# A down projection of seven products in place of eight, with sums of its weights made by accumulating DMAs

## The chip, the cores and the metric

The kernel runs on one core of one Trainium2 chip. The metric is the device time of one launch in microseconds (us), the median of several executions.

## What is computed

One step of a hybrid streaming encoder layer on 640 tokens (512 of a new stream, 8 streams of 16), all in float32, with a model width of 2048:

```python
proj = x @ w_in + b_in                            # 2048 -> 6144: conv and HGRN2 groups
mixed = concat(conv_mixer(proj), hgrn2_mixer(proj)) @ w_out
h = layer_norm(ALPHA * x + mixed)
ffn = (silu(h @ w_gate) * (h @ w_up)) @ w_down    # 2048 -> 5632 -> 2048
y = layer_norm(ALPHA * h + ffn)
```

The conv mixer is a causal convolution of 31 taps over 1024 channels with a carried history; the HGRN2 mixer a gated recurrence of 8 heads with a carried state.

## The kernel before

Channels lie on the partitions and tokens on the free dimension, in two halves of 320 (`TH`). A float32 product is made of three float32r matmuls (`mac`, lines 222 to 227): weights and operand are each split into a high and a low part (`part`, lines 156 and 157: ACT casts the high part, DVE subtracts to get the low one), and high x high, high x low and low x high are added up in PSUM.

Weights come through one feed. `take` gives the next piece of up to 512 columns as four tiles of 128 x 128 and prepares those behind it; `feed_weights` loads up to 1024 columns at a time (`raw`, three buffers, line 206) on SP's queue. The order of TensorE, DVE and ACT is the order of the program text; the orders of POOL and SP are set by a scheduler. After a group of matmuls, `tick` runs steps of side work (mixers, norms).

The stages, one after another on TensorE:

- Input projection, with the mixers as side work. `MIXERS` sets the order: c0 c1 h0 c2 h1 c3 c4 h2 c5 h3 and so on, c for a conv tile and h for a head. For each conv tile POOL clears the head of `u` (line 318), loads the history into a `tmp` buffer (line 320), copies it into `us` (line 321), and later stores the new history (lines 335 to 338). DVE then runs the taps over `u` and `us` (lines 360 and 362). For each head POOL loads the state (line 449), spreads the streams' queries into `qm` (line 542) and stores the new states (lines 563 and 578). The four `tmp` buffers go round among histories, gates, squares (line 580) and normed outputs (line 591).
- Output projection, residual, first norm.
- SwiGLU: the gate and up products in Winograd's form of Strassen's algorithm, seven products of a quarter of the size in place of eight (`quad`); sums of their weights are made on DVE (line 879). Results go to DRAM as `act_d`.
- Down projection, 5632 to 2048, in the plain form: 44 hidden tiles in six chunks (`CHUNKS`). For the first four chunks (`down`), a weight tile serves both halves of the tokens; the last two (`down_half`) go through all 16 output tiles for the first half of the tokens and then again for the second, so their weights are loaded and split twice. The operands of a chunk are loaded from `act_d` on POOL's queue (line 951) and split during the chunk before (`stage`). Sums over the chunks are added to the residual `res`, reloaded from `h_d`, on DVE (lines 1027, 1029, 1052, 1071).
- Second norm (`pivot`, `norm2`), that of the first half under the products of the second.

A semaphore named DMASW0 to DMASW7 belongs to each DMA of POOL's queue in turn, so an issue there waits until the DMA eight before it is done.

Of the kernel before, what the change touches and what calls it, by code (L numbers as in the profile page):

```python
# [10 lines left out]
F32 = mybir.dt.float32  # L11
# [60 lines left out]
def kernel(ctx, tc, xT, cacheT, s_in, w_in, w_out, w_last, w_gate, w_up, w_down,  # L72
# [53 lines left out]
    # Side work (the mixers, the norms) runs after each group of matmuls: a step of each lane, and as many  # L126
    # steps of the fillers as fit in the time (us of VectorE; each step yields what it takes).
# [26 lines left out]
    def part(src, hi, lo, lows=None):  # L154
        """src as hi + lo. lows: takes what VectorE has to do, for later."""
# [8 lines left out]
    # The feed holds, in the order of their use, functions that give up to 512 columns of weights.  # L164
# [7 lines left out]
    def take(ahead=None):  # L172
        """The next weights as (hi, lo) of P columns each; the ones after them are prepared ahead."""
# [22 lines left out]
    def feed_weights(*srcs, offset=2500):  # L196
        """Each up to 1024 columns of weights in all; an item of the feed for each 512."""
        raws = []

        def raw():  # L200
            if not raws:
                with tc.high_priority(offset=offset):
                    t = wp.tile([P, 1024], F32, tag="raw", name="raw")
                    j = 0
                    for src in srcs:
                        nc.sync.dma_start(t[:, j:j + src.shape[-1]], src)
                        j += src.shape[-1]
# [3 lines left out]
        total = sum(src.shape[-1] for src in srcs)  # L211
# [4 lines left out]
    def split(kt, half, src, lows=None):  # L216
        hi = xp.tile([P, TH], F32R, tag=f"xh{kt}_{half}", name="xh")
        lo = xp.tile([P, TH], F32R, tag=f"xl{kt}_{half}", name="xl")
        part(src, hi, lo, lows)
        return hi, lo  # L220
# [30 lines left out]
    def first_pair(outs):  # L251
        """The first two output tiles together, in the order in which x arrives."""
# [49 lines left out]

    mixed = {}
# [72 lines left out]
    def mean_of(t, out, n):  # L376
        """Sum over the partitions / D of the n columns of t, in all partitions."""
# [176 lines left out]
        # states  # L554
# [12 lines left out]
        # outputs, tokens on the partitions  # L567
# [30 lines left out]
    def stream_blocks(t):  # L598
        """The block of LB columns of each stream, out of its own P columns."""
# [212 lines left out]
    # weights^T = [[a11, a12], [a21, a22]] (output tiles x channels), h = [[b11, b12], [b21, b22]]  # L812
# [24 lines left out]
    # What follows the products, a little after each of the next ones: (us of VectorE, function).  # L837
# [15 lines left out]
    def early(store):  # L853
        """The two products that need the first half of the tokens alone."""
# [58 lines left out]
    def quad(stored, c11, c12, c21, c22, upper, lower):  # L913
        """upper, lower: what follows when c11 and c12, when c21 and c22 are there."""
# [22 lines left out]
        for s in range(2):  # L937
            for i in sum(groups, ()):
                product(bank[i], operand[i], s)
                if s == 1:  # L940
                    later.extend(sums.get(i, []))
        later.append((0.7, lower))

    act_d = [dp.tile([P, NTOK], F32, name=f"act_d{ft}") for ft in range(FT)]
# [9 lines left out]
    def split_act(c, i, t):  # L954
        return [split(2 * i + h, c % 2, half(t, h)) for h in range(2)]

    def feed_down(c, n):
        feed_weights(w_down[n, :, P * CHUNKS[c][0]:P * sum(CHUNKS[c])])

    def swiglu(j):  # L960
# [12 lines left out]
        def store(e):  # L973
            vec.tensor_tensor(g[e], g[e], v[e], op=ALU.mult)
            pool.dma_start(act_d[2 * j + e], g[e])

        quad(stored[1], half(v[0], 0), half(v[0], 1), half(v[1], 0), half(v[1], 1),
             lambda: store(0), lambda: store(1))

    acts = []  # L980
    early_d = []
    for wq, stored in products:
        feed_quad(wq, stored)
    for c in range(NCHUNK - 2):
        for n in range(KD):
            feed_down(c, n)
    for h in range(2):
        for c in LAST:
            for n in range(KD):
                feed_down(c, n)  # L990
# [6 lines left out]
    for j in range(QUADS):  # L997
        swiglu(j)

# [1 line left out]
    def down_macs(c, n, outs, halves, between=None):  # L1001
        i = 0
# [244 lines left out]
```

## Time and profile before

| | |
|---|---|
| median of 3 runs | 2798.1 us (2797.22 to 2800.35) |
| profiled execution, span | 2797.9 us |
| TensorE, instructions | 18888 matmuls, each with its weight load |
| DMA, HBM read and written | 302.53 MB and 37.28 MB |
| weights on SP's queue (q1) | 276.42 MB, 31.5% of 16 engines' span |
| POOL's queue (q0) | 63.44 MB, 7.0% |
| loads of w_down | 112 of 512 KB, 16 of 256 KB |

The trace gives for an instruction its start, length, line, output and inputs, and in brackets the idle time of its engine before it with what ended it. PE is TensorE, PEld its weight loads, DVE VectorE, ACT ScalarE, POOL GpSimd, SP SyncE. The profiled execution's own time is not given apart from its span; the runs beside it lie within 2.5 us of that.

### The profile page before, as it was taken

To read this page: it belongs to the slowest core of one execution; us is meant where nothing else is said; L and a number is where in the kernel's file an instruction comes from. 1 tells how busy PE (TensorE), PEld (TensorE's weight loads), DVE (VectorE), ACT (ScalarE), POOL (GpSimd) and SP (SyncE) were. 2 spreads that over 40 slices of the span, in tenths; PEclk is the share of its full clock that TensorE was granted. 3 is DMA by queue.
4 is the path that set the end of the run, shared out by engine and by line. 5 is a ranking of instruction groups with operands and counts; after the bars stand their busy time and mean duration, and the time that the engine had idled before them with its cause. 6 is when DMAs were issued, how large, how long until landed. Compare 5 with 4: busy or idle time off the path is not lost.

```text
span 2797.9 us, 47299 instructions
## 1 busy us (share of the span) xinstructions
PE 2758.8 (99%) x18888; PEld 2740.3 (98%) x18888; DVE 1928.7 (69%) x3461; ACT 1005.1 (36%) x1706; POOL 155.3 (6%) x270
## 2 busy tenths in 40 slices
PE   8999999999999999999999999999999999999996
PEld 8999999999999999999999999999999999999996
DVE  7866876875665667788888777777776423335686
ACT  3222122222543466643333333343334212213444
POOL 1001000000000000100000000000001000000001
PEclk9999999999999999999999999999999999999998
DMA  5222222222225556754454323333336423334463
GB/s 187 65 79 90 64 87 79 82 77 70 74 88 170 173 165 205 259 169 156 158 158 156 107 89 105 102 95 104 99 104 230 135 74 111 97 91 128 140 180 103
DMA packets 104094, 342.89 MB, mean 123 GB/s; under 512 B 12992, under 2 KB 17600, under 8 KB 103872
## 3 DMA queue, kind: packets, MB, share of 16 engines
q1 hardware_dynamic: 87296, 276.42, 31.5%
q0 software_dynamic: 16576, 63.44, 7.0%
q8 instruction: 148, 2.42, 0.4%
q14 instruction: 74, 0.61, 0.1%
HBM read 302.53 MB, written 37.28 MB: 121 GB/s over the span
## 4 chain that ended last, share of the span: by engine, by line
PE 97%; DVE 1%; ACT 1%; DMA 0%; issue 0%; SPq 0%; ACTq 0%; DVEq 0%
PE psg L224 21%; PE psg L227 21%; PE psg L225 21%; PE psd L224 10%; PE psd L227 10%; PE psd L225 10%; PE psh L525 2%; PE psh L565 0%; PE psh L441 0%; PE psh L574 0%; PE psd L1151 0%; PE psh L570 0%; PE psh L504 0%; PE psh L498 0%; PE psh L557 0%; DVE res L1112 0%
## 5 line engine op out<-in xcount | busy, mean ns | idle before, releaser
L224 PE MATMUL psg<-xh,hi 128*128 128x320 f32 x3404 | 1050.1, 313 | 1.2 <-ACT xh L156 1.2
L225 PE MATMUL psg<-xl,hi 128*128 128x320 f32 x3404 | 1037.3, 309 | 1.2 <-DVE xl L157 1.2
L227 PE MATMUL psg<-xh,lo 128*128 128x320 f32 x3404 | 895.3, 310 | 2.9 <-DVE lo L157 2.8
L156 ACT CAST hi<-raw 128x512 fp32r<-128x512 f32 (+1 forms) x824 | 507.2, 619 | 1039.8 <-PE psg L225 715.9
L157 DVE TENSOR_TENSOR lo<-raw,hi 128x512 fp32r<-128x512 f32 (+1 forms) x824 | 560.3, 688 | 293.7 <-ACT hi L156 292.5
L224 PEld LDWEIGHTS psg<-xh,hi 128*128 128x128 f32 x3404 | 640.3, 188 | 4.2 <-issue 1.7
L225 PEld LDWEIGHTS psg<-xl,hi 128*128 128x128 f32 x3404 | 640.2, 188 | 3.9 <-issue 1.7
L227 PEld LDWEIGHTS psg<-xh,lo 128*128 128x128 f32 x3404 | 599.3, 188 | 5.3 <-DVE lo L157 5.2
L225 PE MATMUL psd<-xl,hi 128*128 128x320 f32 x1424 | 436.5, 309 | 0.0
L224 PE MATMUL psd<-xh,hi 128*128 128x320 f32 x1424 | 436.4, 309 | 0.0
L227 PE MATMUL psd<-xh,lo 128*128 128x320 f32 x1424 | 403.6, 309 | 0.0
L156 ACT CAST hi<-S 128x512 fp32r<-128x512 f32 x352 | 218.0, 619 | 356.5 <-PE psd L225 164.3
L157 DVE TENSOR_TENSOR lo<-S,hi 128x512 fp32r<-128x512 f32 x352 | 243.0, 690 | 116.5 <-ACT hi L156 109.7
L224 PEld LDWEIGHTS psd<-xh,hi 128*128 128x128 f32 x1424 | 267.3, 188 | 0.0
L225 PEld LDWEIGHTS psd<-xl,hi 128*128 128x128 f32 x1424 | 267.2, 188 | 0.0
L227 PEld LDWEIGHTS psd<-xh,lo 128*128 128x128 f32 x1424 | 258.1, 188 | 0.0
L224 PE MATMUL psg<-t,hi 128*128 128x320 f32 x624 | 192.8, 309 | 0.0
L225 PE MATMUL psg<-t,hi 128*128 128x320 f32 x624 | 192.8, 309 | 0.0
L227 PE MATMUL psg<-t,lo 128*128 128x320 f32 x624 | 192.8, 309 | 0.0
L362 DVE SCALAR_TENSOR_TENSOR mx<-u,par,mx 128x512 f32<-128x512 f32 x240 | 180.7, 753 | 0.0
L879 DVE TENSOR_TENSOR S<-raw 128x512 f32<-128x512 f32 x176 | 120.7, 686 | 24.8 <-DMA raw<-w_up 14.3
L224 PE MATMUL psd<-t,hi 128*128 128x320 f32 x432 | 133.5, 309 | 0.0
(228 smaller groups left out, 2707.6 us busy)
## 6 DMA issues: line engine op xcount, KB each, us to landing
raw<-w_down SPq DMA_DIRECT2D x112, 512.0 KB, 3.7
raw<-w_in SPq DMA_DIRECT2D x92, 512.0 KB, 3.8
raw<-w_gate SPq DMA_DIRECT2D x88, 512.0 KB, 3.5
raw<-w_up SPq DMA_DIRECT2D x88, 512.0 KB, 3.6
raw<-w_out SPq DMA_DIRECT2D x60, 512.0 KB, 3.9
act_d<-gu POOLq DMA_DIRECT2D x44, 320.0 KB, 2.5
act<-act_d POOLq DMA_DIRECT2D x42, 320.0 KB, 3.8
raw<-w_gate SPq DMA_DIRECT2D x40, 256.0 KB, 3.3
```

Source lines behind the costliest of these rows:

```text
L156: act.copy(hi, src)
L157: low = lambda: vec.tensor_tensor(lo, src, hi.bitcast(F32), op=ALU.subtract)
L224: pe.matmul(ps, w[0], xh, start=start, stop=False)
L225: pe.matmul(ps, w[0], xl, start=False, stop=False)
L227: pe.matmul(ps, w[1], xh, start=False, stop=stop)
L362: vec.scalar_tensor_tensor(y, x, col(w0 + j), y, op0=ALU.mult, op1=ALU.add)
L525: pe.matmul(ps[:, P // 2 * c:P // 2 * (c + 1)], blk(k, c), upper(q, c, m), start=True, stop=True)
L879: vec.tensor_tensor(t, x, y, op=op)
```

## The change

The down projection takes the seven-product form too: `w_down` is seen as pairs of output tiles (p, 0 to 7) by two halves of the hidden tiles (22 each), the activations as two halves of the hidden tiles by two halves of the tokens. The seven products run one after another (`DOWN`), each over all eight p: 22 weight tiles of 128 x 128 for each p, on one half of the tokens' width (320 columns), three matmuls each. Weights of products 1, 2 and 4 are quarters of `w_down`; those of 5, 7, 6 and 3 are sums of two, two, three and four quarters. The operands of a product are loaded from `act_d` (one to three pieces for each two tiles), subtracted on DVE, split, and put where operands of the product before are no longer needed (`prepare`, a filler). Each result is added to one or more quarters of `res` (`done1` and so on).

The sums of weights lie in DRAM (`s_d`). They are made by DMAs on POOL's queue, from DRAM to DRAM: a copy of one term, and then an accumulating DMA that adds another. There are 32 of each, and each is of 128 x 2816 float32. `tick` issues one at every second call, from the first tile of the input projection on.

```diff
-CHUNKS = [(0, 4), (4, 8), (12, 8), (20, 8), (28, 8), (36, 8)]
-NCHUNK = len(CHUNKS)
-LAST = (NCHUNK - 2, NCHUNK - 1)
...
+PAIRS_OUT = KD // 2
+DOWN = (1, 2, 6, 7, 4, 5, 3)
...
         while fillers and credit[0] > 0:
-            credit[0] -= fill()
+            cost = fill()
+            if cost is None:
+                break
+            credit[0] -= cost
+        ticks[0] += 1
+        if ticks[0] % 2:
+            next(summing, None)
+    ticks = [0]
...
+    HALF = QUADS * P
+    s_d = {i: [dp.tile([P, HALF], F32, name=f"s{i}_{p}") for p in range(PAIRS_OUT)] for i in (5, 7, 6, 3)}
+    def quarter_of(p, r, c):
+        return w_down[2 * p + r, :, HALF * c:HALF * (c + 1)]
+    def sum_weights(out, src, accumulate):
+        if accumulate:
+            pool.dma_start(out, src, accum_op=ALU.add, max_dma_last_dim=2 * HALF)
+        else:
+            pool.dma_start(out, src)
+    def weight_sums():
+        for terms in (lambda p: [(5, quarter_of(p, 1, 0), quarter_of(p, 1, 1)),
+                                 (7, quarter_of(p, 0, 0), quarter_of(p, 1, 0))],
+                      lambda p: [(6, s_d[5][p], quarter_of(p, 0, 0))],
+                      lambda p: [(3, s_d[6][p], quarter_of(p, 0, 1))]):
+            for n in range(2):
+                for p in range(PAIRS_OUT):
+                    for i, *two in terms(p):
+                        sum_weights(s_d[i][p], two[n], n == 1)
+                        yield
+    summing = weight_sums()
...
-    def raw_act(c, i):
-        if c == 0 and i < 2:
-            t = gp.tile([P, NTOK], F32, tag="pre", name="pre", bufs=2)
-        else:
-            t = sp.tile([P, NTOK], F32, tag=f"a{i}", name="act", bufs=1)
-        pool.dma_start(t, act_d[CHUNKS[c][0] + i])
-        return t
...
-    def feed_down(c, n):
-        feed_weights(w_down[n, :, P * CHUNKS[c][0]:P * sum(CHUNKS[c])])
+    act_d = [dp.tile([P, 2, NTOK], F32, name=f"act_d{j}") for j in range(QUADS)]
+    t2_d = [dp.tile([P, 2, TH], F32, name=f"t2_d{jj}") for jj in range(QUADS // 2)]
 
     def swiglu(j):
         stored = early_d[2 * j:2 * j + 2] if 2 * j < EARLY else [None, None]
...
+    ops = {i: [] for i in DOWN}
+    progress = [-1, 0, 0]
...
+    def loads(i, jj):
+        parts = {1: ("11",), 2: ("21",), 6: ("22", "12", "11"), 7: ("22", "12"), 4: ("t2", "21"),
+                 5: ("12", "11"), 3: ("22",)}[i]
+        out = []
+        for n, name in enumerate(parts):
+            if n == 0:
+                t = gp.tile([P, 2, TH], F32, tag="pre", name="pre", bufs=2)
+            elif n == 1:
+                t = sp.tile([P, 2, TH], F32, tag="xr", name="pre2")
+            else:
+                t = pair_tmp()
+            if name == "t2":
+                pool.dma_start(t, t2_d[jj])
+            else:
+                pool.dma_start(t, half3(act_d[jj + QUADS // 2 * (int(name[0]) - 1)], int(name[1]) - 1))
+            out.append(t)
+        return out
...
+    def prepare(i):
+        nth = DOWN.index(i)
+        got = deque([loads(i, 0)])
+        yield None
+        for jj in range(QUADS // 2):
+            if jj + 1 < QUADS // 2:
+                got.append(loads(i, jj + 1))
+            t, *others = got.popleft()
+            if i == 6:
+                b12, b11_ = others
+                vec.tensor_tensor(b12, b12, b11_, op=ALU.subtract)
+                yield 0.85
+            for o in others[:1]:
+                vec.tensor_tensor(t, t, o, op=ALU.subtract)
+                yield 0.85
+            if i == 6:
+                pool.dma_start(t2_d[jj], t)
+            while nth and (progress[0] < nth - 1 or jj > 8 and progress[0] == nth - 1 and
+                           (progress[1] < PAIRS_OUT - 1 or progress[2] < 2)):
+                yield None
+            hi, lo = space(), space()
+            act.copy(hi, t)
+            yield None
+            vec.tensor_tensor(lo, t, hi.bitcast(F32), op=ALU.subtract)
+            ops[i].extend((hi[:, e], lo[:, e]) for e in range(2))
+            yield 0.85
...
+    def down_weights(i, p, j, n):
+        w = {1: lambda: quarter_of(p, 0, 0), 2: lambda: quarter_of(p, 0, 1), 4: lambda: quarter_of(p, 1, 1)}
+        return (w[i]() if i in w else s_d[i][p])[:, P * j:P * (j + n)]
+    def runs(i):
+        if i == DOWN[0]:
+            return [(range(q, q + 4), [(j, min(4, QUADS - j)) for j in range(0, QUADS, 4)]) for q in (0, 4)]
+        return [((p,), [(j, min(8, QUADS - j)) for j in range(0, QUADS, 8)]) for p in range(PAIRS_OUT)]
+    def feed_down(i):
+        for group, turns in runs(i):
+            for j, n in turns:
+                step = 2 if n == 4 else 1
+                for p in group[::step]:
+                    feed_weights(*(down_weights(i, p + e, j, n) for e in range(step)))
...
-    def down_macs(c, n, outs, halves, between=None):
-        i = 0
-        while i < CHUNKS[c][1]:
-            for w in take():
-                mac(outs, w, [acts[c][i][h] for h in halves], i == 0, i == CHUNKS[c][1] - 1)
-                i += 1
-            if len(halves) == 2 and i < CHUNKS[c][1]:
-                tick()
-            if between is not None:
-                between()
-                between = None
...
-    def down(c):
-        acts.append([])
-        fillers.append(stage(c + 1))
-        if c == NCHUNK - 3:
-            acts.append([])
-        for n in range(KD):
...
+    def down(i, done, between=None):
+        nth = DOWN.index(i)
+        progress[:] = [nth, 0, 0]
+        if i != DOWN[-1]:
+            fillers.append(prepare(DOWN[nth + 1]))
+        bank = {}
+        for group, turns in runs(i):
+            for p in group:
+                if p % 2 == 0:
+                    banks.reverse()
+                    ps = banks[0]()
+                bank[p] = ps[:, p % 2, :TH]
+                if i == DOWN[0]:
+                    res[p] = xp.tile([P, 2, NTOK], F32, tag=f"mx{p}", name="res")
+                    nc.sync.dma_start(res[p], h_d[p])
+            for j0, n in turns:
+                for p in group:
+                    progress[1] = p
+                    j = j0
+                    while j < j0 + n:
+                        while len(ops[i]) < min(j + 4, QUADS):
+                            fill()
+                        for w in take():
+                            mac([bank[p]], w, [ops[i][j]], j == 0, j == QUADS - 1)
+                            j += 1
+                        progress[2] = j // 2
+                        tick(1.0)
+                        settle()
+                        follow()
+                        if between is not None and p == PAIRS_OUT - 1:
+                            between.popleft()() if between else None
...
+    def done1(p, x):
+        two = res[p].rearrange("p r (h t) -> p r h t", h=2)
+        return [(0.85, lambda r=r, op=op: vec.scalar_tensor_tensor(two[:, r], two[:, r], ALPHA, twice(x),
+                                                                   op0=ALU.mult, op1=op))
+                for r, op in ((0, ALU.add), (1, ALU.subtract))]
+    def done2(p, x):
+        return [add(quarter(p, 0, 0), x)]
+    def done6(p, x):
+        return [add(lower(p), twice(x), cost=0.85), add(quarter(p, 0, 1), x, ALU.subtract)]
+    def done7(p, x):
+        return [add(lower(p), twice(x), ALU.subtract, cost=0.85)]
+    sums0 = []
...
+    for i, done in zip(DOWN, (done1, done2, done6, done7, done4, done5)):
+        down(i, done)
+        if i == 4:
+            follow(1e9)
+            lanes.append(norm2_first(sums0[0]))
+    follow(1e9)
+    lanes.append(pivot())
```

Two places of POOL's queue show where the scheduler put the sums. In the names, `s5_0_90` is the DRAM tile of the sum for product 5 and p = 0 (the last number counts buffers), `s0` the state that a head loads. First the start of the program, before:

```order
L422 MEMSET qm_91 128x1024
L318 MEMSET u_96 128x30
L320 DMA tmp_99<-cacheT 128x240
L318 MEMSET u_535 128x30
L321 COPY us_97<-tmp_99 128x8x30 [waits DMASW0_49]
L124 CAST msk_85<-mraw_318 128x384 [waits DMAHW4_49]
L449 DMA s0_826<-s_in 128x8x128 [waits Pool_49]
```

and after:

```order
L358 MEMSET u_535 128x30
L328 DMA s5_0_90<-w_down 128x2816
L361 COPY us_129<-tmp_131 128x8x30 [waits DMASW0_49]
L328 DMA s7_0_98<-w_down 128x2816
L328 DMA s5_1_91<-w_down 128x2816
L328 DMA s7_1_99<-w_down 128x2816
L328 DMA s5_2_92<-w_down 128x2816
L328 DMA s7_2_100<-w_down 128x2816
L328 DMA s5_3_93<-w_down 128x2816
L123 CAST msk_85<-mraw_332 128x384 [waits DMAHW4_49]
L328 DMA s7_3_101<-w_down 128x2816
L489 DMA s0_830<-s_in 128x8x128 [waits DMASW1_49,Pool_49]
```

Eight copies have moved ahead of the load of the first head's state, seven of them ahead of the first instruction that waits for work of the program's (the cast of the masks); in the program's text the eighth is issued at the fifteenth tick.

The other place is around the conv tile c5 and the head h2, before:

```order
L318 MEMSET u_3697 128x30 [waits DVE_49]
L542 COPY qm_91<-a2_3052 128x8x16 [waits DVE_49,PE_49]
L320 DMA tmp_3700<-cacheT 128x240 [waits DMASW6_49,DMASW5_49,DMASW4_49]
L321 COPY us_3698<-tmp_3700 128x8x30 [waits DMASW6_49]
L563 DMA o_hg_p<-st_3781 128x128 [waits DVE_49]
```

and after:

```order
L326 DMA s3_4_118<-w_down 128x2x1408 [waits DMASW0_49]
L326 DMA s3_5_119<-w_down 128x2x1408 [waits DMASW1_49]
L375 COPY tmp_3075<-u_2785 128x30 [waits DVE_49,Activation_49]
L376 COPY tmp_3075<-us_2786 128x240 [waits DVE_49,Pool_49]
L377 DMA o_conv_p<-tmp_3075 128x30 [waits DMASW2_49,Pool_49]
L378 DMA o_conv_s<-tmp_3075 128x240 [waits Pool_49]
L326 DMA s3_6_120<-w_down 128x2x1408 [waits DMASW4_49]
L326 DMA s3_7_121<-w_down 128x2x1408 [waits DMASW5_49]
L358 MEMSET u_3737 128x30 [waits DVE_49]
L582 COPY qm_123<-a2_3084 128x8x16 [waits DVE_49,PE_49]
L360 DMA tmp_3740<-cacheT 128x240 [waits DMASW6_49,DMASW3_49,DMASW2_49]
L361 COPY us_3738<-tmp_3740 128x8x30 [waits DMASW6_49]
```

All 64 sums now stand ahead of the history of c5; the last of them, `s3_7`, is issued in the text at the 127th of about 184 ticks of the input projection. Ahead of the history of c3 stand 25 copies and 24 accumulations, ahead of that of c4 32 and 24, in the same queue.

More of the change, by code (lines that the diff above doesn't have):

```diff
@@ new lines, in half3 @@
+    def half3(t, h):
+        return t[:, :, TH * h:TH * (h + 1)]
+    def prepare(i):
[24 more added lines that the diff above has]
+            yield 0.85
@@ L1065, in pivot, with quarter @@
-    def pivot(h, sums):
+    after.clear()
+    def quarter(p, r, h):
+        return res[p][:, r, TH * h:TH * (h + 1)]
+    def down(i, done, between=None):
[19 more added lines that the diff above has]
+                        while len(ops[i]) < min(j + 4, QUADS):
+                            fill()
+                        for w in take():
[7 more added lines that the diff above has]
+                            between.popleft()() if between else None
+                    if j == QUADS:
+                        later.extend(done(p, bank[p]))
@@ new lines, in add, with twice, lower @@
+    def add(out, x, i=ALU.add, cost=0.5):
+        return cost, lambda: vec.tensor_tensor(out, out, x, op=i)
+    def twice(x):
+        return x.unsqueeze(1).to_broadcast([P, 2, TH])
+    def lower(p):
+        return res[p][:, 1].rearrange("p (h t) -> p h t", h=2)
+    def done1(p, x):
[3 more added lines that the diff above has]
+                for r, op in ((0, ALU.add), (1, ALU.subtract))]
@@ new lines, with done5, pivot @@
+    first = []
+    def done5(p, x):
+        if p == 0:
+            first.append(sp.tile([P, 2, TH], F32, tag="xr", name="first"))
+        return [add(quarter(p, 1, 1), x), add(quarter(p, 0, 1), x, ALU.subtract),
+                (0.5, lambda: accumulate(first[0][:, 0], quarter(p, 1, 1), p == 0))]
+    def pivot():
+        mean = psg()
+        pe.matmul(mean[:, 0, :TH], ones, first[0][:, 0], start=True, stop=True)
+        m = first[0][:, 1]
+        act.activation(m, mean[:, 0, :TH], AF.Copy, scale=2.0)
+        yield 0.0
+        for p in range(PAIRS_OUT):
+            r = res_pair(p, 1)
+            vec.tensor_tensor(r, r, across(m), op=ALU.subtract)
+            yield 0.85
@@ new lines, with total, square @@
+    for i, done in zip(DOWN, (done1, done2, done6, done7, done4, done5)):
[3 more added lines that the diff above has]
+            lanes.append(norm2_first(sums0[0]))
+    follow(1e9)
+    lanes.append(pivot())
+    sums, squares = pair_sums(), pair_sums()
+    stat = []
+    def total(j, terms, start, stop):
+        for i, t in enumerate(terms):
+            pe.matmul(stat[0][:, j, :TH], ones, t, start=start and i == 0, stop=stop and i == len(terms) - 1)
+    def square(out, x):
+        return 0.0, lambda: act.activation(out, x, AF.Square)
@@ new lines, in done3, with most, sum_up @@
+    def done3(p, x):
+        r = quarter(p, 0, 1)
+        if p == PAIRS_OUT - 1:
+            last.append((r, x))
+            return []
+        pair, sq = res_pair(p, 1), pair_tmp()
+        return [add(r, x), square(sq, pair), (0.85, lambda: accumulate(sums, pair, p == 0)),
+                (0.85, lambda: accumulate(squares, sq, p == 0))]
+    last = []
+    def most():
+        r, sq = quarter(PAIRS_OUT - 1, 1, 1), tmp((P, TH))
+        act.activation(warm, eps, AF.Ln)
+        act.activation(sq, r, AF.Square)
+        def sum_up():
+            stat.append(psd())
+            for j, t, partial in ((0, r, sums), (1, sq, squares)):
+                total(j, [partial[:, 0], partial[:, 1], t], True, False)
+        return sum_up
@@ L1170 @@
+    rest = []
+    down(DOWN[-1], done3, deque([lambda: None, lambda: None, lambda: rest.append(most()),
+                                 lambda: None, lambda: rest.pop()()]))
+    (r, x), sq = last[0], tmp((P, TH))
+    vec.tensor_tensor(r, r, x, op=ALU.add)
+    act.activation(sq, r, AF.Square)
+    total(0, [r], False, True)
+    total(1, [sq], False, True)
+    lanes.append(norm2(1, stat[0], sums, squares))
     while lanes:
```

164 lines of the change are left out of this document (66 added, 98 removed).

## The prediction

> **What bounds the kernel now.** I read the head of the page, then the chain that ended last, then stretches of the span. Of the page, the shares, the DMA row of its 40 slices and the chain:
>
> ```profile
> span 2797.9 us, 47299 instructions
> PE 2758.8 (99%) x18888; PEld 2740.3 (98%) x18888; DVE 1928.7 (69%) x3461; ACT 1005.1 (36%) x1706; POOL 155.3 (6%) x270
> DMA  5222222222225556754454323333336423334463
> PE 97%; DVE 1%; ACT 1%; DMA 0%; issue 0%; SPq 0%; ACTq 0%; DVEq 0%
> ```
>
> TensorE is busy for 99% of the span and is 97% of the chain, so each matmul that goes is time, and each wait that reaches TensorE is time too. GpSimd (POOL) is 6% busy, and the DMA engines 20% to 30% in slices 2 to 13, which is the input projection: the two resources that the change loads. The profiled execution's 2797.9 us and the median run's 2798.1 are 0.2 us apart, so a sum made against the one holds for the other.
>
> Stretches of the span (columns: the stretch and its length, then busy us with counts of PE, PEld, DVE, ACT and POOL, the granted clock, the DMA engines' busy share, GB/s):
>
> ```profile
> 0.00:254.00 254.00, 245.55 (x1702) 242.65 (x1703) 185.22 (x408) 69.04 (x121) 18.65 (x39) 1.00 0.33 104
> 0.00:298.00 298.00, 289.55 (x2003) 286.64 (x2004) 217.28 (x474) 79.15 (x136) 22.98 (x47) 1.00 0.33 104
> 0.00:380.00 380.00, 371.55 (x2585) 367.66 (x2586) 285.37 (x622) 94.94 (x162) 27.03 (x56) 1.00 0.30 95
> 4.00:28.00 24.00, 19.86 (x124) 19.87 (x125) 15.37 (x33) 14.61 (x34) 0.39 (x1) 1.00 0.96 329
> 1000.00:1500.00 500.00, 500.00 (x3403) 499.12 (x3402) 409.08 (x699) 236.28 (x408) 46.17 (x84) 1.00 0.56 181
> 2100.00:2150.00 50.00, 47.64 (x312) 47.05 (x312) 35.35 (x63) 21.25 (x41) 7.00 (x13) 0.97 0.68 249
> 2200.00:2400.00 200.00, 200.00 (x1366) 200.00 (x1365) 72.53 (x117) 46.22 (x87) 8.62 (x16) 1.00 0.33 103
> ```
>
> From 4 to 28 us the DMA engines are full (0.96), and that is 329 GB/s. In the down projection (2200 to 2400) 1366 matmuls take 200 us: 146.4 ns each.
>
> **Gain: the matmuls of the down projection.** Before: 44 hidden tiles x 16 output tiles x 2 halves of the tokens x 3 matmuls = 4224. After: 7 products x 8 pairs x 22 tiles x 3 = 3696. That is 528 fewer, all of 320 columns, at 146.4 ns: **-77.3 us**, wholly on the chain.
>
> What hides the rest of that stage. Weights are no longer shared by two halves, so the splitting into two parts grows from 240 to 308 pieces of 512 columns, and DVE also makes the operands (55 subtractions, 77 low parts, of 640 columns each). One row has the price of a piece, one that of 640 columns (mean ns last before the bar):
>
> ```profile
> L157 DVE TENSOR_TENSOR lo<-raw,hi 128x512 fp32r<-128x512 f32 x237 | 160.6, 688 | 132.0 <-ACT hi L156 131.5
> L1029 DVE TENSOR_TENSOR res<-res,psg 128x640 f32<-128x640 f32 x24 | 19.7, 822 | 59.2 <-PE psg L227 59.2
> ```
>
> 308 x 0.688 = 212 us, 132 x 0.822 = 109 us, and about 120 us for adding seven products to the residual and for the norms: some 440 us of DVE in 3696 x 0.1464 = 541 us, 81%. In 1000 to 1500 us DVE is at 409 of 500, 82%, and TensorE at 500.00 of 500: that share is covered, so I charge nothing. Uncovered it would be the excess of some local queue; I allow 10 us. Loads go from 61 to 81 MB of weights and some 40 MB of operands, 122 MB in 541 us or 226 GB/s, under the 329. The start of the stage lost 2.4 us (50 - 47.64 in 2100 to 2150) and has the same form after; the last norm keeps its steps. Both 0.
>
> **Cost: the sums of weights.** 64 DMAs on POOL's queue, each 128 x 2816 x 4 B = 1.442 MB: 32 copies HBM to HBM and 32 accumulations. The text of the program issues one at every second tick, but the order of POOL's queue has them hoisted, and on the chip POOL waits there for no tick: it stops only when the DMA eight before is not done, or at a row of the mixers. What waits for POOL in before, at these places (start, length):
>
> ```profile
> 224.86 0.57 POOL L321 COPY us<-tmp 128x240 f32<-128x240 f32 x1 [2.18 <-DMA tmp<-cacheT]
> 254.22 0.82 DVE L591 TENSOR_TENSOR tmp<-psh,sm 128x640 f32<-128x640 f32 x1
> 272.73 0.80 POOL L321 COPY us<-tmp 128x240 f32<-128x240 f32 x1
> 298.60 0.48 DVE L362 SCALAR_TENSOR_TENSOR mx<-us,par,mx 128x128 f32<-128x128 f32 x1
> 353.73 0.39 POOL L321 COPY us<-tmp 128x240 f32<-128x240 f32 x1 [2.77 <-DMA tmp<-cacheT]
> 379.30 0.70 ACT L580 ACTIVATE tmp<-psh 128x640 f32<-128x640 f32 x1 [9.42 <-PE psh L574]
> ```
>
> These are three conv tiles (c3, c4, c5). POOL copies a loaded history into `us`; then DVE or ACT goes on: at 254.22 because it takes over the buffer that held the history, at 298 in the taps (the row is their second one), at 379.30 for the buffer again. There is slack of 29, 25 and 25 us. In after, each history load stands on the queue behind 25 copies and 24 accumulations (c3), 32 and 24 (c4), 32 and 32 (c5), and the engines of one queue take them in turn. DVE runs in order, and the low parts of TensorE's weights stand behind the waiting instruction; ACT's high parts likewise. So a late `us` stops TensorE.
>
> How late: all DMA work ahead of the load has to be done, whatever the order. It is the sums plus what the engines did in before until then: 0.33 x 254 = 84 us, 0.33 x 298 = 98, 0.30 x 380 = 114. The first copy goes out at about 3 us. With c us for a copy and a for an accumulation, the delay is
>
> - c3: 3 + 25c + 24a + 84 - 254
> - c4: 3 + 32c + 24a + 98 - 298
> - c5: 3 + 32c + 32a + 114 - 379
>
> and the largest counts, since TensorE, idle in none of these stretches before, can't catch up. The seven copies at the very start delay x, whose load already fills the engines from 4 to 28 us, by up to 7c; this is the same DMA time and is not added again. Nor is the half clock after a stop, since the DMA engines set the pace by then.
>
> No row of before has a transfer from HBM to HBM, nor an accumulation. Bounds: at the least either costs one pass of its bytes at the full rate, 1.442 MB / 329 GB/s = 4.4 us; a copy reads and writes HBM, at most two passes, 8.8 us; an accumulation reads two places and writes one, at most three, 13.1 us. Rows of raw loads and of stores each have only one side in HBM, so they are as near to one end as to the other. I take the middles: c = 6.6, a = 8.8. That gives 209, 225 and 231 us: **+231 us**.
>
> The Trainium skill, DMA: Bandwidth & Descriptors, section "Latency and other measured facts", gives 214 GB/s each way as the full rate of copies between HBM tensors: an estimate of 6.7 us for c, by which the total would be some 3 us higher; no run here shows it yet.
>
> A gain from the sums themselves is excluded: before forms no sums of these weights, so they take no work away. Read back in the down projection they are plain loads like those of w_down:
>
> ```profile
> raw<-w_down SPq DMA_DIRECT2D x112, 512.0 KB, 3.7
> ```
>
> **Sum:** 2797.9 - 77.3 + 231 = 2951.6, so 2952 us. Its own range, at a = 8.8 and c from 4.4 to 8.8: the c5 stop gives 141 + 282 - 262 = 161 and 282 + 282 - 262 = 302, so 2882 to 3023.
>
> **Rivals.**
>
> 1. *One pass each: the sums nearly hide, faster.* If the DMA engine reads and writes at once, and the second source comes free, c = a = 4.4: 49, 49 and 20 us, so 2797.9 - 77.3 + 49 = 2770. For it: a load's packets already read one memory and write another within one pass, and the engines are busy only 0.30 of the first 380 us. Against: three streams at one memory instead of one. It decides at the point where the c4 stop reaches 77 us: with c = a at 56c = 274, c = 4.9 us; above that the kernel is slower. Chance 0.22.
> 2. *An accumulation is twice a copy.* If the second source takes a whole turn of the engine, a = 2c; with c = 6.6 and a at its bound 13.1 the c5 stop gives 211 + 419 - 262 = 368, so 3089. For it: every packet in the rows has one source only. Against: nothing in the trace. Chance 0.23. The Trainium skill, Collectives: The Full Stack, section "The bandwidth ceiling: the fold count and why AG ≠ RS ≠ AR", says that an adding DMA moves about half as fast as a copying one, because it reads two sources through one ring; by that rule this rival holds, and no run here shows it yet.
> 3. *Nothing reaches TensorE.* If POOL's rows have far more slack than 25 us, or the queue lets short loads pass, only the gain is left: 2721. For it: POOL is 6% busy. Against: the three pairs of rows above. Chance 0.05.
>
> My own case has 0.47; 0.03 is left for a time within 0.2% (5.6 us, about what a measurement of this kernel can tell from no change), where the delay happens to be near 77.
>
> **The numbers.** 2952 is the likeliest. The range holds rivals 1 and 2 and the bounds: low 2768 (one pass, 2770, a little less), high with two and three passes, c = 8.8 and a = 13.1: 282 + 419 - 262 = 439, so 3160 with no allowance. Rival 3 and what lies beyond the bounds are left out. Faster: 0.22 + 0.05 = 0.27; same 0.03; slower 0.47 + 0.23 = 0.70.
>
> **What would show it.** Right: the median time of POOL's accumulations to landing far above the 3.7 us (the last figure of the row above) of a load of weights; the DMA row near 9 from the start until 500 us or later; DVE and ACT waiting for POOL's `us` and for DMAs in the input projection, TensorE's idle time there 200 us and more; from the output projection on, the same stage lengths as before; the down projection 77 us shorter at an unbroken TensorE. Wrong: the input projection at its old length with the DMA engines at 0.9 or less (rival 1 or 3); DVE near 100% with TensorE waiting in the down projection (my cover is gone); or TensorE stopped by weight loads rather than by POOL, in which case the same DMA time shows up under another name and the sum still stands.

## The result and the profile after

The changed kernel takes 2918.68 us (median of 4, 2918.45 to 2923.21) against 2799.22 before (2797.22 to 2802.78): 1.0431 times as long, 95% interval 1.0416 to 1.0446. It is slower. The page of its profiled execution, with the lines that answer to those of before:

```profile
span 2916.9 us, 47082 instructions
PE 2722.0 (93%) x18346; PEld 2687.4 (92%) x18346; DVE 1992.8 (68%) x3566; ACT 1070.4 (37%) x1790; POOL 285.9 (10%) x433
PE   5969499999999999999999999999999888898996
PEclk8989799999999999999999999999999999999998
DMA  8999995222222555664444332232326587566563
PE 11%; issue 4%; DVE 2%; DMA 1%; POOL 1%; ACT 0%; DVEq 0%; ACTq 0%; POOLq 0%
```

TensorE's row has two thin places: slices 1 to 5, where the DMA row is full, and slices 32 to 37, the down projection. Between them it is as solid as before. The same places in the stretches (columns as before: length, busy us and counts of PE, PEld, DVE, ACT and POOL, granted clock, DMA share, GB/s):

```profile
70.00:350.00 280.00, 225.12 (x1566) 222.43 (x1564) 164.12 (x360) 51.53 (x79) 50.90 (x66) 0.91 1.03 271
1200.00:1700.00 500.00, 500.00 (x3411) 500.00 (x3410) 420.41 (x724) 214.63 (x366) 45.29 (x83) 1.00 0.50 168
2400.00:2700.00 300.00, 267.01 (x1706) 262.76 (x1705) 174.14 (x268) 112.55 (x189) 49.15 (x72) 0.94 0.65 205
```

In 2400 to 2700 only 1706 matmuls ran; at 146.4 ns they need 249.8 us. So 50 us of 300 are lost, 33 as idle time and 17 to a lower clock, with DVE only 58% busy.

How late the first stage ends is read from a step that both kernels have, the copy into `qm` on POOL (count, shortest, median and longest ns, first and last start). Before, then after:

```profile
L542 POOL COPY qm<-a x8: 708/792/858, 120.1 to 799.0; 128x128 f32<-128x128 f32 x8
```

```profile
L582 POOL COPY qm<-a x8: 706/793/994, 152.2 to 895.8; 128x128 f32<-128x128 f32 x8
```

The last head is 96.8 us late, and 2916.9 - 2797.9 = 119.0 at the end. The next mark is the load of the residual with which the down projection starts (the last two figures are the first and last start). Before, then after:

```profile
L1024 SPq DMA_DIRECT2D res<-h_d x8: 319/481/641, 2120.7 to 2140.4; - x8
```

```profile
L1134 SPq DMA_DIRECT2D res<-h_d x8: 327/377/649, 2217.5 to 2234.3; - x8
```

It is 96.8 us late as well, so nothing is lost or gained between the two marks. So the bill has two parts: +97 in the input projection, where the prediction had +231, and +22 in the down projection and the norm at its end, where it had -77. The second part is 99 us worse than forecast, the first 134 better.

Who waits for whom in the first 600 us, four of the lines (us in all, times, the longest):

```profile
POOL us L361 <- DMA tmp<-cacheT: 120.9, 7, 43.7
PE psh L481 <- DVE tmp L631: 61.2, 2, 38.3
DVE tmp L631 <- DMA s<-s: 44.3, 1, 44.3
DVE tmp L631 <- POOL us L361: 28.9, 1, 28.9
```

TensorE's two stops at L481 are of 22.9 us (until 215.29) and of 38.3. POOL's rows at the longer one (start, length, in brackets the idle time before and its end):

```profile
306.81 0.60 POOL L360 DMA_DIRECT2D tmp<-cacheT  x1 [8.05 <-DMA s<-w_down]
314.36 0.50 POOL L328 DMA_DIRECT2D s<-s  x1 [6.96 <-DMA s<-w_down]
355.01 0.38 POOL L361 COPY us<-tmp 128x240 f32<-128x240 f32 x1 [40.15 <-DMA tmp<-cacheT]
```

and DVE's and TensorE's behind them:

```profile
355.43 0.82 DVE L631 TENSOR_TENSOR tmp<-psh,sm 128x640 f32<-128x640 f32 x1 [44.28 <-DMA s<-s]
356.40 1.30 PE L481 MATMUL psh<-con,tmp 128*128 128x128 f32 x5 [38.29 <-DVE tmp L631]
```

The history of c3, 120 KB, was issued at 306.81 and POOL could copy it at 355.01: 48 us behind sums issued earlier in its queue. The copy ends at 355.39, and DVE, which takes over the history's buffer, starts at 355.43; the profile puts that wait down to a sum's landing. The transposes for which TensorE had waited 38.3 us started at 356.40. The mechanism of the prediction is there, step for step; its size is not. It is not the whole loss either: the first three `qm` copies are late by 32, 59 and 97 us and the other five by 97. The first 32 us are lost before either stop; the second experiment shows by what.

In the down projection TensorE waits for one thing above all (whole span):

```profile
PE psd L236 <- DVE res L1155: 26.4, 14, 4.7
PE psg L236 <- DVE res L1155: 26.2, 14, 5.6
```

Those are 28 waits, all in the second p of a pair (24 of them 12 matmuls into it, 4 of them 24), for an instruction of DVE that adds a finished product to the residual. One of the long ones, on DVE:

```profile
2539.36 0.82 DVE L1072 TENSOR_TENSOR b<-pre,b 128x640 fp32r<-128x640 f32 x1
2544.01 0.82 DVE L1062 TENSOR_TENSOR pre<-pre,pre 128x640 f32<-128x640 f32 x1 [3.82 <-DMA pre<-t_d]
2544.75 1.28 DVE L164 TENSOR_TENSOR lo<-raw,hi 128x512 fp32r<-128x512 f32 x2
...
2548.03 0.81 DVE L1155 TENSOR_TENSOR res<-res,psd 128x640 f32<-128x640 f32 x1
```

and on TensorE:

```profile
2523.81 0.38 PE L236 MATMUL psg<-b,hi 128*128 128x320 f32 x1 [1.00 <-DVE res L1155]
2548.99 0.60 PE L236 MATMUL psd<-b,hi 128*128 128x320 f32 x1 [4.68 <-DVE res L1155]
2574.73 0.61 PE L236 MATMUL psg<-b,hi 128*128 128x320 f32 x1 [3.90 <-DVE res L1155]
```

DVE stops 3.82 us for the load of an operand of the next product, works off what has piled up, and reaches the residual 8 us after its stop began. TensorE starts 0.15 us after the end of that instruction. After the two waits of 3.9 and 4.7 us the first matmul is longer (0.60 and 0.61 against 0.38 us); from 2549 to 2553 us the granted clock is 0.50.

### The profile page after: what moved, and what is told of

It is laid out like the page before. It is cut to its first block, busy times and chain, and to the rows that moved or that the text cites. A ratio compares the mean times of both kernels' runs of the same rounds, so it can differ in the third digit from the quotient of the medians.

```text
span 2916.9 us, 47082 instructions
## 1 busy us (share of the span) xinstructions
PE 2722.0 (93%) x18346; PEld 2687.4 (92%) x18346; DVE 1992.8 (68%) x3566; ACT 1070.4 (37%) x1790; POOL 285.9 (10%) x433
## 5 line engine op out<-in xcount | busy, mean ns | idle before, releaser
L163 ACT CAST hi<-raw 128x512 fp32r<-128x512 f32 (+2 forms) x920 | 554.3, 605 | 1018.0 <-PE psg L237 709.0
L164 DVE TENSOR_TENSOR lo<-raw,hi 128x512 fp32r<-128x512 f32 (+2 forms) x920 | 612.1, 671 | 324.2 <-ACT hi L163 323.2
L236 PE MATMUL psg<-x,hi 128*128 128x320 f32 x2684 | 831.1, 314 | 0.0
L237 PE MATMUL psg<-x,hi 128*128 128x320 f32 x2684 | 819.3, 310 | 0.0
L239 PE MATMUL psg<-x,lo 128*128 128x320 f32 x2684 | 710.1, 310 | 2.9 <-DVE lo L164 2.8
L236 PEld LDWEIGHTS psg<-x,hi 128*128 128x128 f32 x2684 | 506.2, 189 | 2.4 <-issue 1.7
L237 PEld LDWEIGHTS psg<-x,hi 128*128 128x128 f32 x2684 | 506.2, 189 | 2.1 <-issue 1.7
L239 PEld LDWEIGHTS psg<-x,lo 128*128 128x128 f32 x2684 | 474.5, 188 | 5.3 <-DVE lo L164 5.2
L236 PE MATMUL psg<-b,hi 128*128 128x320 f32 x616 | 197.0, 320 | 33.1 <-DVE res L1155 26.2
L236 PE MATMUL psd<-x,hi 128*128 128x320 f32 x736 | 227.4, 309 | 0.0
L237 PE MATMUL psd<-x,hi 128*128 128x320 f32 x736 | 227.4, 309 | 0.0
L239 PE MATMUL psd<-x,lo 128*128 128x320 f32 x736 | 227.4, 309 | 0.0
L236 PE MATMUL psd<-b,hi 128*128 128x320 f32 x616 | 197.3, 320 | 31.9 <-DVE res L1155 26.4
L237 PE MATMUL psd<-b,hi 128*128 128x320 f32 x616 | 194.8, 316 | 0.0
L237 PE MATMUL psg<-b,hi 128*128 128x320 f32 x616 | 194.6, 316 | 0.0
```

The costliest lines, as they stand in the source:

```text
L163: act.copy(hi, src)
L164: low = lambda: vec.tensor_tensor(lo, src, hi.bitcast(F32), op=ALU.subtract)
L236: pe.matmul(ps, w[0], xh, start=start, stop=False)
L237: pe.matmul(ps, w[0], xl, start=False, stop=False)
L239: pe.matmul(ps, w[1], xh, start=False, stop=stop)
```

## The experiments

Twelve kernels, each timed beside the kernel before (2798.15 to 2798.55 us). e1, e2, e3 and e6 leave out work that the result needs; they only show what that work costs. Two theories were to be tested: *theory 1*, that the input projection pays for the place of the sums in POOL's queue and for nothing else, and, for the down projection, *A* against *B*, below. The recorded expectations use the letters in more than one way. In e3 and e4, theory 2 is that DVE and ACT wait for the operands' loads, rival A that they have too much work, and rival B that TensorE waits for DVE to empty PSUM. From e5 on A is the shared PSUM tile and B the late loads. In e9 A is the load issued too late, and C the bandwidth that it takes.

**No sums.**

```diff
-        if ticks[0] % 2:
-            next(summing, None)
...
-        return (w[i]() if i in w else s_d[i][p])[:, P * j:P * (j + n)]
+        return w.get(i, w[1])()[:, P * j:P * (j + n)]
```

> Leaves out the 64 sums of weights; the products that used them read a quarter of w_down instead. Theory 1 (the sums' DMA time, queued ahead of the conv histories, is what delays the input projection): the qm copy of head h2 is back at 350 us from 446 and the time falls by the 97 us of that delay, to 2822 (2810 to 2830). Rival (the delay comes from somewhere else in the change, and the sums only fill idle engines): no change, over 2900.

2823.82 us, ratio 1.0092 (1.0077 to 1.0107): 95 us come back, and no more. The other loss has nothing to do with the DMAs that make the sums: from the first load of the residual to the end this run takes 700.1 us, the changed kernel 699.4 (before: 677.2).

**Copies in place of accumulations.**

```diff
-            pool.dma_start(out, src, accum_op=ALU.add, max_dma_last_dim=2 * HALF)
+            pool.dma_start(out, src)
```

> Makes each of the 32 accumulations a plain copy of the same bytes, so the sums are not formed. Theory 1 with an accumulation at 7.0 us of all engines and a copy at 4.0: the delays of c3, c4, c5 become 29, 27 and about 0, so the time falls by about 70 us, to 2848 (2835 to 2860). Rival (an accumulation costs what a copy costs, and the delay comes from the number of DMAs queued): no change, over 2905.

2857.28 us, ratio 1.0203 (1.0179 to 1.0226). 64 copies cost 33 us where 32 copies and 32 accumulations cost 95. The prices follow from POOL's queue (packets, MB, share of the 16 engines) in the first 550 us of three kernels, before, with 64 copies, and the changed one:

```profile
q0 software_dynamic: 2448, 7.07, 4.7%
```

```profile
q0 software_dynamic: 10048, 99.21, 50.4%
```

```profile
q0 software_dynamic: 13666, 97.79, 67.7%
```

(0.504 - 0.047) x 550 / 64 = **3.93 us** for a copy. Then (0.677 - 0.047) x 550 - 32 x 3.93 = 220.7, and 220.7 / 32 = **6.9 us** for an accumulation.

Where the 33 us of this run lie bears on theory 1. Its `qm` copies, and one of TensorE's waits in the changed kernel, which starts alike (up to 160 us):

```profile
L582 POOL COPY qm<-a x8: 706/790/857, 151.7 to 830.8; 128x128 f32<-128x128 f32 x8
```

```profile
PE psh L236 <- ACT x L163: 21.0, 4, 10.9
```

The first copy of this run is already 31.6 us late (120.1 before) and the last 31.8 (799.0 before): no stop at a history is left. The time is lost at the start, where TensorE waits for casts of `x` and of weights. `x` is loaded on SP's queue, not on POOL's, and took 9.7 us from issue to landing here and 10.1 in the changed kernel, against 4.6 before and 4.3 without the sums. So "for nothing else" does not hold: copies hoisted to the head of the program also slow SP's loads. In the changed kernel these 32 us do not come on top of the 97, for by the prediction's formula c3's history lands when all DMA work ahead of it is done.

**Operands loaded once for each product.**

```diff
-            if jj + 1 < QUADS // 2:
-                got.append(loads(i, jj + 1))
-            t, *others = got.popleft()
+            t, *others = got[0]
...
-            if i == 6:
+            if i == 6 and jj == 0:
                 pool.dma_start(t2_d[jj], t)
```

> In the down projection each product's operands are loaded once instead of eleven times; all subtractions, casts and low parts stay, on the same data again. Theory 2 (DVE and ACT, in order, stand waiting for the operand loads, and TensorE's weights stand behind them): most of the 99 us by which the stages after the input projection miss the forecast come back: 2918 - 80 = 2838 (2825 to 2860). Rival A (DVE and ACT have too much work there): no change, over 2905. Rival B (TensorE waits for DVE to empty PSUM, as the trace names it): no change, over 2905.

2856.0 us, ratio 1.0207 (1.0192 to 1.0222): 63 of the 99 us. DVE and ACT have all their work still. What is left are waits at the same places, now short ones, between 2240 and 2800 us:

```profile
PE psd L236 <- DVE res L1153: 19.2, 14, 4.0
PE psg L236 <- DVE res L1153: 13.6, 13, 1.7
```

**One more tick between preparation steps**, so that an operand's load has longer to land.

```diff
+            if nth:
+                yield None
             t, *others = got.popleft()
```

> From the second product on, each step that prepares operands waits one more tick between asking for the next operands and using the ones asked for before: three ticks (5.3 us) a step in place of two (3.5 us), nothing else. Theory 2: a load of 4.8 us from issue to landing now has the time, and 50 to 75 us come back: 2845 to 2870. Rivals A and B: no change, over 2905, or worse.

2902.93 us, ratio 1.037 (1.0353 to 1.0387): a miss, 16 us in place of some 50 to 75. In the program the next load is issued only when DVE has released a buffer, so I take it that a slower pace moves the load as well as the step that needs it; between 2240 and 2700 us DVE still waited for `act_d` 16 times, 25.4 us (12 times and 16.4 us in the changed kernel, at the same line of the step).

**A PSUM tile for each p.** Why should TensorE wait for a residual that it does not need? The wait sits 12 matmuls into the second p of a pair. Two p's share one PSUM tile, one half each; DVE reads the first p's half while TensorE writes the second's. The halves do not overlap, but the wait is set for the tile. That is theory A; the rival B is that TensorE would stop anyway, for the low parts that the same late DVE makes.

```diff
-                if p % 2 == 0:
+                if p % 2 == 0 or i != DOWN[0]:
                     banks.reverse()
                     ps = banks[0]()
-                bank[p] = ps[:, p % 2, :TH]
+                bank[p] = ps[:, p % 2 if i == DOWN[0] else 0, :TH]
```

> Every p of products two to seven gets a PSUM tile of its own; in the changed kernel p and p + 1 share one, and the program makes TensorE wait, 12 matmuls into p + 1, for VectorE's read of p's half of that tile, though the halves do not overlap. Theory A (this shared tile is what lets VectorE's lateness reach TensorE): the waits put down to DVE res go (26.4 + 26.2 us), and the half-clock windows that follow the long ones with them (27 us): 2840 to 2870 us. Rival B (the operands' loads make VectorE late, and TensorE would only stop a little later, for the split weights from the same VectorE): the wait comes back as ACT hi or DVE lo, 2900 to 2919 us.

2873.62 us, ratio 1.027 (1.0255 to 1.0285): 45 us, just short of what A alone was to give. The waits for a product's `res` are gone from TensorE's list, and part of B is true as well, for low parts are waited for in their place:

```profile
PE psg L239 <- DVE lo L164: 16.2, 17, 2.5
PE psd L239 <- DVE lo L164: 13.9, 21, 3.6
```

**Both: a tile for each p, and operands loaded once.** The two edits above together.

> e5_own_psum with the operands of each product of the down projection loaded once instead of eleven times as well, and T2 stored once (wrong operands, the same work on VectorE and ScalarE). Without the tile of its own this took 2856.0. Theory A: the loads only lengthen the waits at the shared tile, so with the tile apart they are worth little: within 15 us of e5_own_psum. Rival B: the loads are the cause, so this is 40 us or more below e5_own_psum. If both act, some 36 us (the waits left without loads) come off 2856: 2820.

2812.1 us, ratio 1.0049 (1.0033 to 1.0066). In the down projection TensorE waits for 1.7 us in all; one stretch of it:

```profile
2400.00:2500.00 100.00, 100.00 (x684) 100.00 (x683) 76.28 (x117) 46.73 (x79) 1.42 (x2) 1.00 0.53 156
```

The two losses add: 45 us for the shared tile, 63 for the loads, 107 for both, about what was missing (99). At 76% DVE holds nothing up, as the prediction had it, once nothing makes it late. Each of A and B is true of a part.

**The sums moved into SwiGLU**, each pair held back by a 16-byte write of a SwiGLU result into its buffer (`gate` is the result just added up):

```diff
+            pool.dma_start(s_d[i][p][0:1, 0:4], gate[0:1, 0:4])
+            sum_weights(s_d[i][p], one, False)
+            sum_weights(s_d[i][p], two, True)
```

> The same 64 sum transfers, but each pair (copy and accumulation) behind a 16-byte write of a SwiGLU result into its buffer, so that they run through SwiGLU, two pairs per set of seven products, and none stands ahead of a convolution history on the queue. Theory 1 (the input projection pays because the history loads and copies stand behind the sums in one queue): the 97 us come back and SwiGLU hides the transfers (22 us of DMA work in about 68): 2815 to 2835 us. Rival (354 us of transfer work costs its share wherever it runs, by holding up weight loads): 2860 to 2920 us.

3021.84 us, ratio 1.0794 (1.0778 to 1.081): a clear miss, 103 us more than the changed kernel. The input projection did come back (last `qm` copy at 799.0), but SwiGLU does not hide the sums: from there to the first load of the residual 1518.0 us pass, 1321.7 before. DVE's waits between 1100 and 2250 us:

```profile
DVE S L914 <- DMA raw<-w_gate: 100.7, 29, 5.6
DVE S L914 <- DMA raw<-w_up: 83.3, 19, 7.1
DVE gu L991 <- DMA s<-gu: 43.7, 6, 13.8
DVE gu L961 <- DMA act_d<-gu: 40.5, 5, 14.6
```

and of the changed kernel between 1000 and 2150 us:

```profile
DVE S L919 <- DMA raw<-w_up: 12.3, 10, 2.6
DVE S L919 <- DMA raw<-w_gate: 9.8, 11, 2.4
```

Weights come late (184 us of waiting in place of 22; the DMA engines were busy 0.79 of 1200 to 1700 us, against 0.50), and 84 us are of my making: the small write that holds a sum back reads a SwiGLU buffer, and with the stores it stands in POOL's queue behind the sums before. The two were not separated.

**The last two together** (tile for each p, sums in SwiGLU):

> e7_gated_sums and e5_own_psum together. Theories 1 and A: the gains add, 2919 - 97 - 50 to 80 = 2742 to 2772 us, below the kernel before. Rivals (either one): 2800 or more.

2972.74 us, ratio 1.0621 (1.0605 to 1.0637): 49 us under e7, so the shared tile's 45 hold there too; the rest is e7's.

**Operands loaded two steps ahead**, with the tile for each p:

```diff
-                t = gp.tile([P, 2, TH], F32, tag="pre", name="pre", bufs=2)
+                t = gp.tile([P, 2, TH], F32, tag="pre", name="pre", bufs=3)
...
-        got = deque([loads(i, 0)])
+        ahead = 1 if i == 6 else 2
+        got = deque(loads(i, jj) for jj in range(ahead))
...
```

> e5_own_psum (2873.6), and the operands of the down projection loaded two preparation steps ahead instead of one (three buffers for the first operand, a ring of four for the second; five of the seven products; the room comes from the ring of mixed SwiGLU weights, four instead of five). Theory A (VectorE is late because it waits in order for a load that was issued too shortly before): most of the 61 us between e5 and e6 come back, 2815 to 2845 us. Rival C (the transfers take bandwidth from the down projection's own weights, whenever they are issued): 2860 to 2880 us.

2839.67 us, ratio 1.0155 (1.0138 to 1.0172): 34 of the 61 us between e5 and e6, inside what A gave. C, that bandwidth alone does it, is out: as many bytes are loaded, only earlier. The other 27 are not settled; 15 of them lie between 2150 and 2400 us, around the stage's start (TensorE 234.61 of 250 us, DMA share 0.67), where the first product's weights and the second's operands are loaded together. In e6, with each product's operands loaded once, TensorE was busy for 250.00 of these 250 us at a share of 0.51, so that part too goes with the loads; whether by their number or by their lateness is open.

**The sums spread over input and output projection**, held back by a value that DVE copies from PSUM: a pair (copy and accumulation) for every third product of the input projection, two for every step of the output projection.

> The changed kernel with each pair of sum transfers held back by a 16-byte write of a value that VectorE has just copied from a product's PSUM: one pair for every third product of the input projection, two for every step of the output projection. 2 copies and 1 accumulation stand ahead of the first head's copy and 16 and 8 ahead of c6, where it was all 64 from c5 on. Theory 1 (position in the one queue): the 97 us come back, 2815 to 2840 us. Rival (transfer work costs its time wherever it runs, as it did in SwiGLU in e7): 2900 us or more.

2951.26 us, ratio 1.055 (1.0534 to 1.0566): a miss in the total, and the best evidence that a load behind sums in POOL's queue stops TensorE. The input projection runs as before:

```profile
70.00:350.00 280.00, 279.95 (x1969) 277.75 (x1968) 211.17 (x458) 61.47 (x95) 31.50 (x52) 1.00 0.49 137
```

and the new loss, 128 us, lies between the last `qm` copy and the first load of the residual, most of it at one place of the output projection (waits from 700 to 1200 us):

```profile
PE psg L236 <- DVE lo L161: 88.5, 22, 68.4
DVE res L751 <- DMA xr<-xT: 83.9, 2, 70.0
```

`xr`, the input for the residual, is loaded on POOL's queue as well. Its load was issued at 988.51 us, after POOL had been busy with sums, and with waiting for them, since 931.99; DVE waited 70 us for it, and TensorE 68 for DVE. A new place, the same mechanism.

**e9 and e10 together:**

> e9_ahead_own and e10_spread_sums together. If theories 1 and A hold both: 2715 to 2750 us, below the kernel before (2798). If only one does: 2800 us or more.

2872.33 us, ratio 1.027 (1.0255 to 1.0286): 79 us under e10, the same as e9 under the changed kernel (79). The stop in the output projection is still there.

**e9 with all sums in the input projection**, two pairs for every three products, held back in the same way:

```diff
+        if pairs_of_sums and (calls[0] % 3 or calls[0] == 21):
+            i, p, one, two = pairs_of_sums.popleft()
+            gate = cp.tile([1, 4], F32, tag="gate", name="gate", bufs=4)
+            vec.tensor_copy(gate, ps[0:1, 0:4])
+            pool.dma_start(s_d[i][p][0:1, 0:4], gate)
+            sum_weights(s_d[i][p], one, False)
+            sum_weights(s_d[i][p], two, True)
```

> e9_ahead_own (2839.7), and all 32 pairs of sum transfers held back as in e10 but inside the input projection, two pairs for every three products, so that none stands near the output projection's residual loads (in e10 VectorE waited for such a load for up to 70 us); 35 copies and 17 accumulations ahead of c5's history where it was all 64. Theory 1 (a load that is needed stands behind sums in the one queue): the input projection runs as before and the 97 us come off, 2735 to 2765 us, below the kernel before. Rival (bandwidth: 352 us of transfers in some 480 us, beside weights that took 0.24 of the engines): weight loads come late and 20 us or more stay, 2770 to 2840 us.

2745.64 us (5 runs, 2744.98 to 2748.44), ratio 0.9815 (0.9802 to 0.9829): 1.85% faster than the kernel before, with the whole interval below 1, and faster than the changed one by 173 us.

```profile
70.00:350.00 280.00, 279.95 (x1969) 277.74 (x1968) 210.82 (x465) 61.46 (x95) 42.16 (x67) 1.00 0.73 193
350.00:550.00 200.00, 199.95 (x1399) 197.74 (x1398) 146.15 (x326) 45.67 (x70) 42.34 (x49) 1.00 0.73 201
2400.00:2700.00 300.00, 298.85 (x2024) 296.94 (x2023) 214.11 (x342) 147.98 (x252) 33.10 (x48) 1.00 0.67 210
```

The same sums, with the engines at 0.73, cost the input projection nothing (279.95 and 199.95 us busy); the last `qm` copy is back at 799.2 us. In the down projection 2024 matmuls run where 1706 ran. The span of 2743.9 stands 23 us above 2797.9 - 77.3 = 2720.6: 17 of them between 2150 and 2400 us, where e9 lost 15.

## Why the prediction came out where it did

2952 was forecast, 2918.7 measured: the sign and the range held. But that the total is near is luck: two terms were wrong in opposite directions, by 134 and by 99 us.

- *The gain of 77.3 us* is right. With the down projection free of waits (e6) 684 matmuls take 100 us, 146.2 ns each, and e6 stands 13.6 us above the kernel before (2798.47 beside it), where -77.3 + 96.8 gives 19.5.
- *The mechanism of the cost* is right: the queue's order, the history's load, `us`, DVE in its order, TensorE. e1 gives back 95 of 97 us, e10 and e12 show the input projection free of loss once the sums stand elsewhere in the same queue, and e10 moves the stop to another load of that queue. The delay of `x` at the start was named too, as up to 7c, which is 27.5 us at c = 3.93; it was 32, and the copies of `qm` bear out that it is not to be added again.
- *Its size* is one step that failed: c = 6.6 and a = 8.8 were taken, 3.93 and 6.9 measured. The formulas were good: with these prices c3 gives 3 + 98 + 166 + 84 - 254 = 97, c4 94 and c5 84, and the largest is what was measured, 96.8. The bound below was itself wrong: 4.4 us came from 329 GB/s, the rate of loads into SBUF, and a copy within HBM took less than that. A bound from the nearest rows held only for the kind of transfer in those rows. The Trainium skill, DMA: Bandwidth & Descriptors, section "Latency and other measured facts", has 214 GB/s each way for copies of 128 x 16 KiB between HBM tensors, an estimate of 6.7 us for a copy here; the measurement, 1.442 MB in 3.93 us or 367 GB/s, decides.
- *Rival 1* (one pass each) was near for the copies (3.93 to 4.4) and wrong for the accumulations. *Rival 2* was near in its ratio and wrong in its base: 6.9 / 3.93 = 1.76 times a copy. The rule beside it (the Trainium skill, Collectives: The Full Stack, section "The bandwidth ceiling: the fold count and why AG ≠ RS ≠ AR": in a ring of several cores the adding step runs about half as fast as the copying one, because it reads two sources) agrees with the trace to that extent. *Rival 3* is out.
- *"That share is covered, so I charge nothing"* is the other step that failed, by 99 us; "I allow 10 us" was far too little. The share was right: DVE was at 81% in the sum and at 76% in e6, with TensorE hardly stopped. What failed is the inference from a share to a cover. From 1000 to 2150 us of the changed kernel DVE waited only 22 us for transfers; in the down projection it runs, in order, behind loads issued one step earlier, and each late load delays everything after it. And the residual's addition, counted as covered work of 120 us, carried a wait for TensorE that the diff brought in with the pairing of two p's in one tile. The prediction looked at neither.
- *"The start of the stage lost 2.4 us and has the same form after"*: not so. From 2150 to 2300 us, until half of the first product is done, TensorE is idle for 17.4 us in the changed kernel, waiting for the high and low parts of weights; from 2150 to 2400 for 17.3 even in e12.
- A slip that changes nothing: the loads of w_down before are 62.9 MB by the sizes in the table (1024 bytes to a KB), not 61.

Of the signs named for "wrong", the one that came, TensorE waiting in the down projection, was tied to DVE near 100%. It came with DVE at 58%: an engine that serves in order can hold up another while it is idle itself.

## What to carry to other kernels

A low busy share is cover only for work whose inputs are there; before an engine is called free, list what its in-order instructions wait for, and how far ahead those loads are issued. A queue is an order: long transfers with no deadline belong behind every short one that something waits for, and the program text does not decide that where a scheduler does, so tie them to a value that exists only at the right time. Take one that nobody needs back: in e12, with copies kept for this alone, DVE waited for none of the small writes, in e10 once, 6.7 us; in e7 a SwiGLU buffer served, and DVE waited 84 us for small writes and stores. Two results that share a PSUM tile can share its waits, as here, even where their halves never touch.

## What the runs showed of the hardware

- An HBM to HBM copy moves 1.442 MB in 3.93 us of all engines (367 GB/s), faster than the 329 GB/s at which the loads of the kernel's start ran with the engines at 0.96. An accumulation of the same size takes 6.9 us.
- The same 64 transfers cost 97 us, 0 us or about 196 us by their place: at the head of the queue in the input projection; spread over that stage with the engines at 0.73; in SwiGLU, where the weights' loads are waited for (a part of it by the way they were held back).
- Waits of TensorE can cost more than their length. After one of 1.0 us the next matmul took 0.38 us, after 4.7 and 3.9 us 0.60 and 0.61; the granted clock over 2400 to 2700 us is 0.94, and 17 us go with it beside 33 of idle time. Which wait brings the low clock is not settled: after 2.17 us (until 2450.83) the clock was 0.60 over the next 4 us, after 2.27 us (until 2408.80) it stayed at 1.00, and after 4.03 us (until 2478.08) the first matmul took 0.39 us and the clock was 0.95 up to 2479 and 0.50 from there to 2482.
